# Output projection by halves of 512 columns, with the weights of a half kept for all token tiles

## The chip, the cores and the metric

The kernel runs on one core of a Trainium2 chip. The metric is the device time of one execution in microseconds; the time before is the median of three runs. The core has five engines: TensorE (PE in the profile, with PEld for its weight loads), VectorE (DVE), ScalarE (ACT), GpSimd (POOL) and SyncE (SP), which here issues most DMA transfers.

## What is computed

One layer of a diffusion backbone on 1280 tokens: 1024 latent tokens and 256 context tokens, each a row of 1024 numbers. All of it is float32. The part that matters, cut from the reference:

```
gates = sigmoid(br_pre).reshape(B, T, N_BRANCH, D_MODEL)
merged = sum(gates * branches, axis=2)
x = x + gt1 * (merged @ w_out)                      # output projection, 1024 x 1024
u2 = rmsnorm(x, g_norm2) * (1 + sc2) + sh2          # normalise rows, scale and shift columns
x = x + gt2 * (square(relu(u2 @ w_ff1)) @ w_ff2)    # feed-forward, 1024 -> 4096 -> 1024
```

`gt1`, `sc2`, `sh2` and `gt2` differ between latent and context tokens. Each float32 operand of a projection is split into two parts, high and low, and a product takes three matmuls: high x high, low x high, high x low.

## The kernel before

The tokens form ten tiles of 128 rows, in three groups: tiles 0 to 3 (group 0), 4 to 7 (group 1), both latent, and 8 and 9 (group 2, the context). A large buffer `z` of 20 pieces of 512 columns (`zs(0)` to `zs(19)`) holds the residual rows during the projection: tile i, called `xt[i]`, is `zs(2i)` and `zs(2i+1)`. In the feed-forward stage the same pieces hold weights and results, so a piece must have been stored (`scr_x`) and read by the normalising before it is overwritten.

Stages around the change, in order:

1. The merge (lines 963 to 993) sums three gated branches into `z`, and lines 1010 to 1016 split the sums into `mT[k][g]`, for eight blocks k of 128 columns and three groups.
2. `project_out(g, quarters)` multiplies a group with quarters of 256 columns of `w_out`. For each group and quarter anew, `out_weights` loads four halves of 256 KB and splits them (`load_half`: cast on ACT, subtraction on DVE); each holds two blocks k. A token tile of a quarter is 24 matmuls of 256 columns into one PSUM buffer `po` of three, then an eviction: a multiplication by the gate and an addition to the rows on DVE (lines 1090 and 1092), and a sum of squares on ACT (line 1093) into `fsq`. After the fourth quarter the tile is stored to `scr_x`.
3. `modulate_ff(g)` normalises a group: it adds up the squares (line 1039), takes the power -0.5 on POOL (line 131), scales the rows into `xn` (lines 1051 and 1053; six buffers `tmp2`, each for two tiles of a quarter), transposes them on PE (line 1059) and applies scale and shift. For latent groups this gives `u2r` (`raw2`), and splits `u2h` and `u2l`, which make up the quarter blocks B11, B21 (both of group 0) and B22; for group 2 it gives `u2c`.
4. The feed-forward's first product is done with a Strassen-like scheme of seven products for a pair of weight blocks (class `Pair`, 16 pairs). `begin` multiplies with B11 and B21 (two products, named `fB`, of 12 matmuls), `contexts` does the context tokens (48 matmuls of 256 columns, named `fc`), and `rest` multiplies with the sums T4, T2, T3, T1 (named `fT`) and with B22. `quarter_sums` forms these sums on DVE by 16 subtractions in place, and `split_sum` splits each of them.

The order before is: group 0 whole, a quarter of group 1, `modulate_ff(0)`, the rest of group 1, half of group 2, `modulate_ff(1)`, the quarter sums and the split of T4, the other half of group 2; then the begins of pairs 0 and 1, `modulate_ff(2)`, the other sums, the contexts.

The written order is only a priority. A planner with its own model of times places each instruction on its engine when its operands and a buffer are there in that model; on the chip each engine then runs its list in order. Buffers come from pools: 59 of 512 columns (`slot`), which hold `gt1` (4), `mT` (40) and later `u2r`, `u2h`, `u2l`, `u2c` and the split sums; six `six` and six `ring`, for high and low halves of weights; four `first4`; six `tmp2`. A buffer returns to its pool after its last reader.

Of the kernel before, what the change touches and what calls it, by code (L numbers as in the profile page):

```python
# [20 lines left out]
GROUPS = ((0, 512), (512, 512), (1024, 256))  # L21
# [28 lines left out]
def hybrid_step(  # L50
# [8 lines left out]
    V, A, G, PE = engines  # L59
    SP = nc.sync  # L60
# [15 lines left out]
    def ps_mm(name):  # L76
        return pp.tile([P, 512], F32, tag="mm", name=name, bufs=3)
# [79 lines left out]
    xt = [z[:, i * D : (i + 1) * D] for i in range(NT)]  # L157
# [90 lines left out]
    V, A, G, PE = (Pinned(tc, e) for e in engines)  # L248
# [73 lines left out]
    for g in range(3):  # L322
        t0, n = GROUPS[g]
# [91 lines left out]
    for g in range(3):  # L415
        t0, n = GROUPS[g]
# [291 lines left out]
    def quarter_sums(raw):  # L708
        for kk in range(4):
            b11, b21, b12, b22 = raw["B11"][kk], raw["B21"][kk], raw["B12"][kk], raw["B22"][kk]  # L710
            if raw is u_raw:
                for t, k, g in ((b11, kk, 0), (b12, kk, 1), (b22, kk + 4, 1), (b21, kk + 4, 0)):
                    SP.dma_start(t, scr_u[g][k])
            for out, x, y in ((b11, b12, b11), (b12, b22, b12), (b22, b22, b11), (b21, b22, b21)):
                V.tensor_tensor(out, x, y, ALU.subtract)

    def split_sum(dst, raw, nm):
        for kk in range(4):
            t = raw[SUMS[nm]][kk]
            if nm == "T2" and kk < 3:  # L720
                hi, lo = (six(f"t2{i}{kk}") for i in "hl")
            else:
                hi, lo = slot(f"{nm}h{kk}"), slot(f"{nm}l{kk}")
            A.copy(hi, t)
            V.tensor_tensor(lo, t, hi.bitcast(F32), ALU.subtract)
            dst[nm, kk] = hi, lo
# [87 lines left out]
    def load_half(src, name):  # L814

        raw = first4(f"raw_{name}", F32)
        SP.dma_start(raw, src)
        hi, lo = six(f"hi_{name}"), ring(f"lo_{name}")
        A.copy(hi, raw)  # L819
        V.tensor_tensor(lo, raw, hi.bitcast(F32), ALU.subtract)  # L820
        return hi, lo
# [141 lines left out]
    for ri, r in enumerate(ORDER):  # L963
        scr = (scr_ya, scr_yb, scr_yc)[r]
        ys = [[] for _ in range(4)]
        for g in range(3):
            for kc in range(4):
                t0, n = GROUPS[g]
# [4 lines left out]
        for d in range(KT):  # L973
            if d % 2 == 0:
                wb = [load_half(w_branch[r, d // 2][:, i * 512 : i * 512 + 512], f"wb{r}_{d}_{i}") for i in range(2)]
            for g in range(3):
                t0, n = GROUPS[g]
# [25 lines left out]
        return tl  # L1003

    gt1 = bcast_rows(0, "gt1")
    def out_weights(g, q):
        return [load_half(w_out[q, i // 2][:, i % 2 * 512 : i % 2 * 512 + 512], f"wo{g}{q}_{i}") for i in range(4)]

    first_out = out_weights(0, 0)
    mT = [[] for _ in range(KT)]  # L1010
    for g in range(3):
        for k in range(KT):
# [16 lines left out]
    raw2 = [[None] * KT for _ in range(2)]  # L1029
    u2s, u2c = {}, [None] * KT  # L1030
    scr_x = [dp.tile([P, D], F32, name=f"scr_x{i}") for i in range(NT)]

    fsq = cp.tile([P, NT, 4], F32, name="fsq")

    def modulate_ff(g):
        t0, n = GROUPS[g]
        tiles = range(t0 // P, (t0 + n) // P)
        fs = small([P, 4], f"fs{g}")[:, : len(tiles)]
        V.reduce_sum(fs, fsq[:, tiles[0] : tiles[-1] + 1, :], axis=mybir.AxisListType.X)
        r = rstd_of(fs, len(tiles), f"f{g}")  # L1040

        j = 1 if g == 2 else 0
        for qt in range(4):
            xn = []
            for ii, i in enumerate(tiles):
                if ii % 2 == 0:
                    t = tmp2(f"xn{i}_{qt}")
                v = t[:, (ii % 2) * 256 : (ii % 2) * 256 + 256]
                xv = xt[i][:, qt * 256 : (qt + 1) * 256]
                if ii % 2 == 0:  # L1050
                    A.activation(v, xv, AF.Copy, scale=r[:, ii : ii + 1])
                else:
                    V.tensor_scalar(v, xv, r[:, ii : ii + 1], None, ALU.mult)
                xn.append(v)
            for kk in range(2):
                k = qt * 2 + kk
                ps = ps_sd(f"pt2{g}_{k}")
                for ii in range(n // P):
                    PE.transpose(ps[:, ii * P : (ii + 1) * P], xn[ii][:, kk * P : (kk + 1) * P], ident)
                if g == 2:  # L1060
                    c = slot(f"u2{k}c")
                    u2c[k] = hi, lo = c[:, 0:256], c[:, 256:512]
                    A.activation(ps[:, :n], ps[:, :n], AF.Identity, bias=sh2[:, k, j : j + 1], scale=a2[:, k, j : j + 1])
                    V.tensor_copy(hi, ps[:, :n])
                    V.tensor_tensor(lo, ps[:, :n], hi.bitcast(F32), ALU.subtract)
                    continue
                rf = raw2[g][k] = slot(f"u2r{k}_{g}", F32)
                A.activation(rf, ps[:, :n], AF.Identity, bias=sh2[:, k, j : j + 1], scale=a2[:, k, j : j + 1])
                if g == 0 or k >= 4:
                    hi, lo = slot(f"u2h{k}_{g}"), slot(f"u2l{k}_{g}")  # L1070
                    V.tensor_copy(hi, rf)
                    V.tensor_tensor(lo, rf, hi.bitcast(F32), ALU.subtract)
                    u2s[f"B{1 + k // 4}{1 + g}", k % 4] = hi, lo

    def project_out(g, quarters=range(4)):
        t0, n = GROUPS[g]
        for q in quarters:
            wq = first_out if (g, q) == (0, 0) else out_weights(g, q)
            for i in range(t0 // P, (t0 + n) // P):
                o = i * P - t0  # L1080
                ps = ps_mm(f"po{q}_{i}")
                for k in range(KT):
                    whi, wlo = wq[k // 2]
                    s = slice((k % 2) * 256, (k % 2 + 1) * 256)
                    mh, ml = mT[k][g]
                    PE.matmul(ps[:, :256], mh[:, o : o + P], whi[:, s], start=k == 0, stop=False)  # L1086
                    PE.matmul(ps[:, :256], ml[:, o : o + P], whi[:, s], start=False, stop=False)  # L1087
                    PE.matmul(ps[:, :256], mh[:, o : o + P], wlo[:, s], start=False, stop=k == KT - 1)  # L1088
                gt = gt1[(2 if g == 2 else 0) + q // 2][:, (q % 2) * 256 : (q % 2) * 256 + 256]
                V.tensor_tensor(ps[:, :256], ps[:, :256], gt, ALU.mult)  # L1090
                xq = xt[i][:, q * 256 : (q + 1) * 256]
                V.tensor_tensor(xq, xq, ps[:, :256], ALU.add)  # L1092
                A.activation(ps[:, 256:512], xq, AF.Square, accum_out=fsq[:, i, q : q + 1])  # L1093
                if q == 3:
                    SP.dma_start(scr_x[i], xt[i])


    project_out(0)
    project_out(1, (0,))
    modulate_ff(0)  # L1100
    project_out(1, (1, 2, 3))
    project_out(2, (0, 1))
    modulate_ff(1)
    quarters = (("B11", 0, 0), ("B21", 0, 4), ("B12", 1, 0), ("B22", 1, 4))
    raw2q = {nm: raw2[g][o : o + 4] for nm, g, o in quarters}
    quarter_sums(raw2q)
    split_sum(u2s, raw2q, "T4")
    project_out(2, (2, 3))

# [47 lines left out]
    pairs = {}  # L1159

    def feed_pair(fp):
        odd = fp % 2
        pairs[fp] = FeedPair(
            f"{fp}", fp, (w_ff1[2 * fp], w_ff1[2 * fp + 1]), 4 if odd else 0, range(8, 12) if odd else range(12, 16), u2s, u2c)

    for fp in (0, 1):
        feed_pair(fp)
        pairs[fp].begin()
    modulate_ff(2)
    for nm in ("T3", "T2", "T1"):  # L1170
        split_sum(u2s, raw2q, nm)
    for fp in (0, 1):
# [174 lines left out]
def _layout(inputs):  # L1347
    import numpy as np

    f = {k: np.asarray(v) for k, v in inputs.items()}  # L1350
    a = {}
# [11 lines left out]
    s = np.arange(P)  # L1363
# [31 lines left out]
    a["w_gate"] = wgt.transpose(1, 0, 2)  # L1395
    a["bg"], a["m0"] = bg, m0
    a["w_branch"] = f["w_branch"][0].reshape(3, 4, P, 4, 256).transpose(0, 3, 2, 1, 4).reshape(3, 4, P, 1024)
    a["w_out"] = f["w_out"][0].reshape(2, 4, P, 4, 256).transpose(3, 0, 2, 1, 4).reshape(4, 2, P, 1024)
    a["w_ff1"] = f["w_ff1"][0].reshape(KT, P, NFF, P).transpose(2, 1, 0, 3).reshape(NFF, P, D)
    a["w_ff2"] = f["w_ff2"][0].reshape(NFF, P, D)  # L1400
    a["w_pool"] = f["w_pool"][0].transpose(1, 0, 2)
# [45 lines left out]
```

## Time and profile before

| what | value |
|---|---|
| median of three runs | 1984.17 us (1979.58 to 1986.23) |
| the profiled execution | 1989.21 us |
| its span, first to last instruction | 1987.4 us |
| PE busy | 1923.3 us, 97% |
| PEld busy | 1656.8 us, 83% |
| DVE busy | 1332.6 us, 67% |
| ACT busy | 858.1 us, 43% |
| mean granted TensorE clock | 0.989 |
| casts and subtractions of `w_out` | 48 of each, 28.8 us of ACT and 32.2 us of DVE |

"Busy" is the time in which an engine has an instruction under way. Matmuls overlap one another, so the pace of PE is read from the starts of successive instructions. The granted clock is the share of full speed that PE was given in a stretch. A bracket behind an instruction gives the idle time of its engine before it and what ended it. Times in rows are microseconds from the start of the span.

### The profile page before, as it was taken

The page shows a single profiled execution, that of the slowest core. Times are in us where ns is not written, and L with a number is a line of the kernel's source. Part 1 is how long each engine was busy: PE and PEld are TensorE (multiplying, and loading weights), DVE is VectorE, ACT ScalarE, POOL GpSimd, SP SyncE. Part 2 cuts the span into 40 slices and gives each one's busy share as a digit, 9 for nine tenths or more (in the row PEclk, how much of TensorE's full clock was granted, in tenths as well). Part 3 has the DMA queues.
Part 4 walks back from the last instruction along what each step waited for, and adds up shares of the span by engine and source line. Part 5 has one row for each costly group of instructions (what it writes and reads, how often), then busy time and mean ns, then how long its engine had stood idle before and what let it go on. Part 6 is the DMA issues. An engine that isn't in the chain of part 4 may idle for free. (4 is left out here: it accounts for less than half of the span.)

```text
span 1987.4 us, 29215 instructions
## 1 busy us (share of the span) xinstructions
PE 1923.3 (97%) x10544; PEld 1656.8 (83%) x10544; DVE 1332.6 (67%) x2269; ACT 858.1 (43%) x1780; POOL 382.5 (19%) x372
## 2 busy tenths in 40 slices
PE   5999999999899999999999999999999999999997
PEld 2788888998778888878889998888888878888886
DVE  6684344448878979774566689888776654654664
ACT  6543454653143333331014565554445544443443
POOL 3000001116402324330000005445441110000002
PEclk9999999999999999999999998999999999999999
DMA  8211111112564545469634535776774586655544
GB/s 341 86 45 38 48 59 42 40 57 85 175 228 145 169 142 176 133 210 345 234 122 149 170 139 186 271 260 237 249 275 142 190 324 210 197 177 155 165 134 148
DMA packets 160642, 332.70 MB, mean 167 GB/s; under 512 B 18929, under 2 KB 41329, under 8 KB 158449
## 3 DMA queue, kind: packets, MB, share of 16 engines
q1 hardware_dynamic: 107280, 224.30, 34.6%
q10 hardware_dynamic: 38976, 52.97, 7.4%
q0 software_dynamic: 14240, 53.56, 7.3%
q8 instruction: 83, 1.36, 0.3%
q14 instruction: 63, 0.51, 0.1%
HBM read 229.53 MB, written 101.22 MB: 166 GB/s over the span
## 5 line engine op out<-in xcount | busy, mean ns | idle before, releaser
L1155 POOL TENSOR_TENSOR z<-z 128x512 f32<-128x512 f32 x64 | 98.7, 1543 | 133.7 <-DMA z<-in_w_ff 131.0
L885 DVE TENSOR_TENSOR z<-z 128x512 f32<-128x512 f32 x112 | 92.2, 824 | 2.5
L445 POOL PARTITION_ALL_REDUCE acc<-acc x16 | 55.0, 3474 | 188.5 <-DVE acc L439 117.6
L439 DVE SCALAR_TENSOR_TENSOR acc<-z,scond,acc 128x512 f32<-128x512 f32 x112 | 85.9, 815 | 0.0
L1269 POOL TENSOR_TENSOR rs_y<-rs_y,neghalf 128x1 f32<-128x1 f32 x10 | 9.4, 940 | 333.6 <-DVE rs_y L1268 333.6
L1121 ACT ACTIVATE z<-z 128x512 f32<-128x512 f32 x64 | 40.5, 632 | 76.4 <-DVE z L894 36.7
L910 ACT ACTIVATE z<-z 128x512 f32<-128x512 f32 x48 | 30.2, 632 | 71.8 <-DVE z L894 27.7
L819 ACT CAST hi_wb<-raw_wb 128x512 fp32r<-128x512 f32 x24 | 14.8, 620 | 100.7 <-PE pb L987 67.2
L131 POOL TENSOR_TENSOR rs_h<-rs_h,neghalf 128x4 f32<-128x4 f32 (+1 forms) x12 | 11.9, 992 | 207.9 <-DVE rs_h L130 207.8
L992 DVE TENSOR_TENSOR sg<-pb,sg 128x512 f32<-128x512 f32 (+1 forms) x48 | 28.9, 602 | 33.0 <-PE pb L988 31.6
L582 DVE SCALAR_TENSOR_TENSOR yc<-th,ccol,z 128x512 f32<-128x512 f32 (+1 forms) x12 | 7.9, 660 | 57.2 <-PE th L580 57.2
L1122 ACT ACTIVATE z<-z 128x512 f32<-128x512 f32 x64 | 40.3, 630 | 1.1
L670 POOL TENSOR_TENSOR z<-z 128x1024 f32<-128x1024 f32 (+13 forms) x20 | 34.8, 1750 | 14.0 <-ACT z L654 12.5
L819 ACT CAST hi_wo<-raw_wo 128x512 fp32r<-128x512 f32 x48 | 28.8, 616 | 19.9 <-PE po L1087 13.6
L1090 DVE TENSOR_TENSOR po<-po,gt 128x256 f32<-128x256 f32 x40 | 17.2, 430 | 29.3 <-PE po L1088 29.2
L1146 POOL DMA_DIRECT2D scr_s<-x x48 | 26.3, 551 | 52.0 <-DVE x L1140 47.3
L446 POOL TENSOR_TENSOR acc<-acc,bt 1x512 f32<-1x512 f32 x16 | 23.8, 1500 | 59.0 <-issue 59.0
L820 DVE TENSOR_TENSOR lo_wo<-raw_wo,hi_wo 128x512 fp32r<-128x512 f32 x48 | 32.2, 686 | 3.6 <-ACT hi_wo L819 3.6
L44 PE MATMUL pm<-wah,shl 128*4 128x512 f32 x32 | 14.7, 479 | 17.2 <-DVE s_x L44 12.5
L1093 ACT ACTIVATE po<-z 128x256 f32<-128x256 f32 x40 | 15.4, 385 | 36.9 <-DVE z L1092 35.7
L516 DVE SCALAR_TENSOR_TENSOR z<-z,dmb,kv 128x129 f32<-128x129 f32 x56 | 16.3, 344 | 21.9 <-PE kv L505 21.6
L569 DVE TENSOR_TENSOR den<-den,gcol 128x2 f32<-128x2 f32 x40 | 6.2, 159 | 35.2 <-ACT den L568 34.4
(5091 smaller groups left out, 7466.7 us busy)
## 6 DMA issues: line engine op xcount, KB each, us to landing
z<-in_w_ff SPq DMA_DIRECT2D x64, 512.0 KB, 5.5
z<-in_w_ada SPq DMA_DIRECT2D x64, 256.0 KB, 3.3
scr_t<-z POOLq DMA_DIRECT2D x16, 1024.0 KB, 4.6
z<-in_w_in SPq DMA_DIRECT2D x24, 512.0 KB, 4.4
scr_g<-z ACTq DMA_DIRECT2D x48, 256.0 KB, 2.0
sg<-scr_g SPq DMA_DIRECT2D x48, 256.0 KB, 4.6
raw_wo<-in_w_out SPq DMA_DIRECT2D x48, 256.0 KB, 3.5
scr_h<-z ACTq DMA_DIRECT2D x48, 256.0 KB, 4.0
```

The source lines that it names most:

```text
L439: V.scalar_tensor_tensor(acc[j], raw, scond[:, k, j : j + 1], acc[j], ALU.mult, ALU.add)
L445: G.partition_all_reduce(acc[j], acc[j], P, bass.bass_isa.ReduceOp.add)
L670: eng.tensor_tensor(at(dst, a, b), at(src, a - l, b - l), at(src, a + r_, b + r_), ALU.add)
L819: A.copy(hi, raw)
L820: V.tensor_tensor(lo, raw, hi.bitcast(F32), ALU.subtract)
L885: V.tensor_tensor(out, x, y, op)
L910: A.activation(t, t, AF.Sigmoid)
L992: V.tensor_tensor(sg[:, :n], pb[:, :n], sg[:, :n], ALU.mult)
L1121: A.activation(t, t, AF.Relu)
L1122: A.activation(t, t, AF.Square)
L1146: G.dma_start(scr_s[fp][:, i, :], t)
L1155: G.tensor_tensor(out, x, y, ALU.subtract)
```

## The change

The projection is cut into two halves of 512 columns instead of quarters of 256. All eight blocks of a half are loaded and split once, and stay for all ten token tiles: 16 loads of 256 KB instead of 48. A tile of a half is 24 matmuls of 512 columns. The array `w_out` is laid out to match.

The blocks of the first half lie in `six`, `ring` and `first4`, those of the second in eight slots (k below 4) and again in `six` and `ring`; the raw weights pass through `tmp2`. The order becomes: half 0 of tiles 0 to 9, half 1 of tiles 0 to 4, `modulate_ff(0)`, half 1 of tiles 5 to 9; then `begin` of pair 0, `modulate_ff(1)`, `begin` of pair 1, `modulate_ff(2)`, the quarter sums and all four split sums, the contexts.

In `z`, even pairs now use pieces 0 to 3 for weights and 4 to 7 for results (group 0's rows), odd pairs 8 to 11 and 12 to 15 (group 1's rows). Before, weights of pairs 0 and 1 lay in group 0's pieces and their results in group 1's. `FREE`, the order in which the second product takes pieces over, is changed to suit.

```diff
-    def out_weights(g, q):
-        return [load_half(w_out[q, i // 2][:, i % 2 * 512 : i % 2 * 512 + 512], f"wo{g}{q}_{i}") for i in range(4)]
-    first_out = out_weights(0, 0)
+    def out_weights(hf, ks=range(KT)):
+        ws = []
+        for k in ks:
+            raw = tmp2(f"raw_wo{hf}_{k}")
+            SP.dma_start(raw, w_out[hf, k])
+            if hf == 0:
+                rooms = (six, ring) if k < 6 else (first4, first4)
+            else:
+                rooms = (slot, slot) if k < 4 else (six, ring)
+            hi, lo = (room(f"{x}_wo{hf}_{k}") for room, x in zip(rooms, ("hi", "lo")))
+            A.copy(hi, raw)
+            V.tensor_tensor(lo, raw, hi.bitcast(F32), ALU.subtract)
+            ws.append((hi, lo))
+        return ws
+    w_out0 = out_weights(0)
...
-    def project_out(g, quarters=range(4)):
-        ...
+    def project_out(hf, wo, tiles):
+        for i in tiles:
+            g = min(i // 4, 2)
+            o = i * P - GROUPS[g][0]
+            ps = ps_mm(f"po{hf}_{i}")
+            for k in range(KT):
+                whi, wlo = wo[k]
+                mh, ml = mT[k][g]
+                PE.matmul(ps, mh[:, o : o + P], whi, start=k == 0, stop=False)
+                PE.matmul(ps, ml[:, o : o + P], whi, start=False, stop=False)
+                PE.matmul(ps, mh[:, o : o + P], wlo, start=False, stop=k == KT - 1)
+            V.tensor_tensor(ps, ps, gt1[(2 if g == 2 else 0) + hf], ALU.mult)
+            xh = xt[i][:, hf * 512 : hf * 512 + 512]
+            V.tensor_tensor(xh, xh, ps, ALU.add)
+            A.activation(ps, xh, AF.Square, accum_out=fsq[:, i, hf : hf + 1])
+            if hf == 1:
+                SP.dma_start(scr_x[i], xt[i])
-    project_out(0)
-    project_out(1, (0,))
+    project_out(0, w_out0, range(8))
+    w_out1 = out_weights(1, range(4))
+    project_out(0, w_out0, (8, 9))
+    w_out1 += out_weights(1, range(4, KT))
+    project_out(1, w_out1, range(5))
     modulate_ff(0)
-    project_out(1, (1, 2, 3))
-    project_out(2, (0, 1))
-    modulate_ff(1)
-    quarters = ...
-    quarter_sums(raw2q)
-    split_sum(u2s, raw2q, "T4")
-    project_out(2, (2, 3))
+    project_out(1, w_out1, range(5, 10))
...
-            ..., 4 if odd else 0, range(8, 12) if odd else range(12, 16), u2s, u2c)
-    for fp in (0, 1):
-        feed_pair(fp)
-        pairs[fp].begin()
+            ..., 8 if odd else 0, range(12, 16) if odd else range(4, 8), u2s, u2c)
+    feed_pair(0)
+    pairs[0].begin()
+    modulate_ff(1)
+    quarters = ...
+    feed_pair(1)
+    pairs[1].begin()
     modulate_ff(2)
+    quarter_sums(raw2q)
+    split_sum(u2s, raw2q, "T4")
     for nm in ("T3", "T2", "T1"):
         split_sum(u2s, raw2q, nm)
-    FREE = (0, 2, 16, 18, 12, 14, 4, 6, 8, 10)
+    FREE = (0, 2, 16, 18, 4, 6, 8, 10, 12, 14)
-    a["w_out"] = ....reshape(2, 4, P, 4, 256).transpose(3, 0, 2, 1, 4).reshape(4, 2, P, 1024)
+    a["w_out"] = ....reshape(KT, P, 2, 512).transpose(2, 0, 1, 3)
```

More of the change, by code (lines that the diff above doesn't have):

```diff
@@ L1038, in modulate_ff @@
         fs = small([P, 4], f"fs{g}")[:, : len(tiles)]
-        V.reduce_sum(fs, fsq[:, tiles[0] : tiles[-1] + 1, :], axis=mybir.AxisListType.X)
+        V.reduce_sum(fs, fsq[:, tiles[0] : tiles[-1] + 1, 0:2], axis=mybir.AxisListType.X)
         r = rstd_of(fs, len(tiles), f"f{g}")
@@ L1073, in modulate_ff @@
                     u2s[f"B{1 + k // 4}{1 + g}", k % 4] = hi, lo
-    def project_out(g, quarters=range(4)):
[L1076 to L1095, printed above, removed]
@@ L1098, in hybrid_step @@
-    project_out(0)
-    project_out(1, (0,))
-    modulate_ff(0)
-    project_out(1, (1, 2, 3))
-    project_out(2, (0, 1))
-    modulate_ff(1)
-    quarters = (("B11", 0, 0), ("B21", 0, 4), ("B12", 1, 0), ("B22", 1, 4))
-    raw2q = {nm: raw2[g][o : o + 4] for nm, g, o in quarters}
-    quarter_sums(raw2q)
-    split_sum(u2s, raw2q, "T4")
-    project_out(2, (2, 3))
+    def project_out(hf, wo, tiles):
[15 more added lines that the diff above has]
+                SP.dma_start(scr_x[i], xt[i])
@@ L1163, in feed_pair @@
         pairs[fp] = FeedPair(
-            f"{fp}", fp, (w_ff1[2 * fp], w_ff1[2 * fp + 1]), 4 if odd else 0, range(8, 12) if odd else range(12, 16), u2s, u2c)
-    for fp in (0, 1):
-        feed_pair(fp)
-        pairs[fp].begin()
+            f"{fp}", fp, (w_ff1[2 * fp], w_ff1[2 * fp + 1]), 8 if odd else 0, range(12, 16) if odd else range(4, 8), u2s, u2c)
+    feed_pair(0)
+    pairs[0].begin()
+    modulate_ff(1)
+    quarters = (("B11", 0, 0), ("B21", 0, 4), ("B12", 1, 0), ("B22", 1, 4))
+    raw2q = {nm: raw2[g][o : o + 4] for nm, g, o in quarters}
+    feed_pair(1)
+    pairs[1].begin()
     modulate_ff(2)
+    quarter_sums(raw2q)
+    split_sum(u2s, raw2q, "T4")
     for nm in ("T3", "T2", "T1"):
@@ L1397, in _layout @@
     a["w_branch"] = f["w_branch"][0].reshape(3, 4, P, 4, 256).transpose(0, 3, 2, 1, 4).reshape(3, 4, P, 1024)
-    a["w_out"] = f["w_out"][0].reshape(2, 4, P, 4, 256).transpose(3, 0, 2, 1, 4).reshape(4, 2, P, 1024)
+    a["w_out"] = f["w_out"][0].reshape(KT, P, 2, 512).transpose(2, 0, 1, 3)
     a["w_ff1"] = f["w_ff1"][0].reshape(KT, P, NFF, P).transpose(2, 1, 0, 3).reshape(NFF, P, D)
```

## The prediction

> **What bounds the kernel now.** I read the totals of the page first, then the stages of the trace around the output projection, and then TensorE (PE) instruction by instruction where a stage shows less than full work.
>
> ```profile
> span 1987.4 us, 29215 instructions
> PE 1923.3 (97%) x10544; PEld 1656.8 (83%) x10544; DVE 1332.6 (67%) x2269; ACT 858.1 (43%) x1780; POOL 382.5 (19%) x372
> ...
> core 0: us, PE busy (x) PEld busy (x) DVE busy (x) ACT busy (x) POOL busy (x), PEclk, DMA share, GB/s
> 1040.00:1060.00 20.00, 20.00 (x116) 17.65 (x115) 14.97 (x26) 7.08 (x13) 1.58 (x3) 1.00 0.27 79
> 1080.00:1100.00 20.00, 20.00 (x169) 20.00 (x169) 10.86 (x23) 7.59 (x22) 0.00 (x0) 1.00 0.41 132
> 1160.00:1180.00 20.00, 20.00 (x172) 20.00 (x171) 18.73 (x41) 17.00 (x38) 0.00 (x0) 1.00 0.27 90
> 1180.00:1200.00 20.00, 15.89 (x73) 13.03 (x72) 18.30 (x41) 14.19 (x30) 1.67 (x1) 0.86 0.33 117
> 1200.00:1220.00 20.00, 19.65 (x123) 18.42 (x122) 18.96 (x37) 12.90 (x27) 10.85 (x6) 0.88 0.40 145
> ```
>
> PE is busy 97% of the span, so time can go only where PE gets fewer microseconds of work, or where it idles or runs slowly. Both occur here. Through the projection (1060 to 1180) PE has no gap, and weight loads (PEld) fill all 20 us of a stage, unlike before it (17.65). At 1180 to 1220 PE has its only hole hereabouts, VectorE (DVE) is nearly full (18 to 19 of 20 us) and the granted clock falls to 0.86 and 0.88.
>
> The next rows are single PE instructions in order of time: start, duration, name.
>
> ```profile
> 1057.66 0.28 PE L1086 MATMUL po<-hi_wo,m0h 128*128 128x256 f32 x1
> ...
> 1175.09 0.28 PE L1086 MATMUL po<-hi_wo,m0c 128*128 128x256 f32 x1
> 1180.73 0.28 PE L1088 MATMUL po<-lo_wo,m7c 128*128 128x256 f32 x1
> 1180.85 0.40 PE L828 MATMUL fB<-u2h,a_0h 128*128 128x512 f32 x1
> 1191.53 0.39 PE L830 MATMUL fB<-u2h,a_1l 128*128 128x512 f32 x1
> 1195.66 2.39 PE L1059 MATMUL pt<-cst,xn 128*128 128x128 f32 x10 [3.74 <-ACT xn L1051]
> 1217.04 0.40 PE L828 MATMUL fT<-t2h,s_0h 128*128 128x512 f32 x1
> ```
>
> Between 1175.09 and 1180.73 lie 47 steps without a gap: 0.120 us per 256-column matmul. Between 1180.85 and 1191.53 lie 47 steps: 0.227 us per 512-column one. The bracket is the hole: PE waited 3.74 us for the normalised rows `xn` of the third token group. What the clock did then:
>
> ```profile
> 1190.00:1195.00 5.00, 1.92 (x9) 1.26 (x7) 4.51 (x10) 3.87 (x7) 1.61 (x1) 0.96 0.14 52
> 1195.00:1200.00 5.00, 3.97 (x16) 3.35 (x17) 3.80 (x12) 4.59 (x11) 0.06 (x1) 0.50 0.66 205
> 1200.00:1205.00 5.00, 5.00 (x26) 5.00 (x25) 3.96 (x12) 2.24 (x5) 3.32 (x3) 0.52 0.15 61
> 1205.00:1210.00 5.00, 4.65 (x37) 4.36 (x36) 5.00 (x6) 4.21 (x10) 2.76 (x3) 1.00 0.28 120
> ```
>
> After the hole the clock stays near 0.5 for about 10 us: 26 instructions where the next 5 us hold 37. The Trainium skill, page "TensorE: Matmul & The Clock Gate", section "Part 1: The HAM clock gate", gives half clock after an idle window of about 3.4 us; the 3.74 us row agrees.
>
> Why the rows came late, in rows of DVE, ScalarE (ACT) and GpSimd (POOL):
>
> ```profile
> 1186.74 0.41 DVE L1092 TENSOR_TENSOR z<-z,po 128x256 f32<-128x256 f32 x1
> 1187.38 0.38 ACT L1093 ACTIVATE po<-z 128x256 f32<-128x256 f32 x1
> 1190.68 0.15 DVE L1039 TENSOR_REDUCE fs<-fsq 128x2 f32<-128x8 f32 x1
> 1193.16 0.16 DVE L130 TENSOR_SCALAR rs_f<-fs 128x2 f32<-128x2 f32 x1
> 1193.39 1.68 POOL rs_f L131
> ```
>
> The last projection matmul starts at 1180.73, but its addition comes 6 us later, the sum of squares waits until 1190.68 and the 0.16 us scaling until 1193.16. DVE is full of quarter sums and splits planned in between.
>
> **The loss of the old tail.** From 1057.66 to 1217.04, 159.4 us, PE does 960 projection matmuls (115.2 at 0.120), 80 transposes at 0.109 (20 take 2.18, row below; 8.7), 48 matmuls of the pairs' first two products (10.9 at 0.227), 96 of the context parts (256 columns, 11.5) and 12 of the T4 product (2.7): 149.0. So 10.4 us are lost: 3.7 in the hole, about 4 to the slow clock, the rest in sub-microsecond waits and switches.
>
> ```profile
> 1116.47 2.18 PE pt L1059 x20
> ...
> 1057.40:1217.03 159.63, 117.97 (x960) 115.90 (x960) 33.67 (x80) 20.34 (x80) 0.97 0.47 161
> 1057.40:1217.03 159.63, 12.76 (x80) 10.23 (x80) 5.75 (x16) 15.79 (x24) 0.97 0.47 161
> 1057.40:1217.03 159.63, 15.28 (x96) 14.50 (x96) 1.15 (x3) 0.97 0.47 161
> 1057.40:1217.03 159.63, 3.36 (x12) 2.16 (x13) 0.00 (x0) 0.58 (x1) 0.97 0.47 161
> ```
>
> (Each row counts one kind of product: projection, transposes, context, T products.)
>
> **The change, part by part.**
>
> Columns: 960 matmuls of 256 become 480 of 512. 115.2 minus 480 x 0.2272 (109.1) is 6.1 us, all on PE, which has no gap there. This is the safest term. Its ends are 5 and 7 us, from reading the steps as 0.118 to 0.120 and 0.226 to 0.228. The clock page's section "Back-to-back issue gap" states another price: columns / 2.4 GHz plus 2.5 ns, thus 109.2 and 215.8 ns, so 480 x 2.5 ns, 1.2 us by estimate. The rows show 13 to 14 ns per matmul beyond the columns instead of 2.5, at both widths, so I stay with the rows.
>
> Weights: 48 loads of 256 KB with a split each become 16.
>
> ```profile
> L819 ACT CAST hi_wo<-raw_wo 128x512 fp32r<-128x512 f32 x48 | 28.8, 616 | 19.9 <-PE po L1087 13.6
> L820 DVE TENSOR_TENSOR lo_wo<-raw_wo,hi_wo 128x512 fp32r<-128x512 f32 x48 | 32.2, 686 | 3.6 <-ACT hi_wo L819 3.6
> L1090 DVE TENSOR_TENSOR po<-po,gt 128x256 f32<-128x256 f32 x40 | 17.2, 430 | 29.3 <-PE po L1088 29.2
> ```
>
> That frees 19.2 us of ACT and 21.5 of DVE, and 8 MB of transfers on SP's queue. Under a full PE this is worth nothing by itself; it pays where DVE was full. Evictions go from 40 of 256 to 20 of 512 columns, three buffers deep, under 5.45 us of matmuls per tile (24 x 0.227): nothing, as about 2.3 us of chain fits thrice. If that cover went, each tile would show a wait of up to 1 us.
>
> Start of the stage: two of the eight first weights (k = 4, 5) take buffers which the merge frees only at its end, 1057.6, and k = 4 is needed 12 x 0.227 = 2.7 us later. A cast (0.62) and a subtraction (0.69) each, in parallel on two engines, take about 2 us, but DVE is 15 of 20 us busy then. Bounds 0 to 2 us; I take 0.5, since the planner can start a second tile meanwhile. The second half's k = 4 to 7 reuse the buffers of k = 0 to 3, free after tile 9 has read each: 5.45 us tile, then 2.7, against four splits at 0.69: hidden, price 0 to 1.
>
> Group 0's normalising moves to about 1137 (14 tiles of 5.45 us from 1057.7, then an eviction and the statistics), under the five remaining tiles (27 us): hidden. Pair 0's weights follow it; before, all four feed-forward loads went out early:
>
> ```profile
> 1119.27 1.43 SPq L843 DMA_DIRECT2D z<-in_w_ff  x3
> 1159.69 2.50 ACT L1051 ACTIVATE xn<-z,rs_f 128x256 f32<-128x256 f32 x6
> 1169.23 0.50 ACT L1051 ACTIVATE xn<-z,rs_f 128x256 f32<-128x256 f32 x1
> z<-in_w_ff SPq DMA_DIRECT2D x64, 512.0 KB, 5.5
> ```
>
> The tail is where I choose. The projection now ends near 1057.7 + 109.1 + 3.5 (32 transposes) + 1 = 1171. Tile 7 ends about 11 us before that (tiles 8 and 9), so group 1's rows are ready near 1164.5, 7 us ahead of the end, where before it was 1159 against 1181. Pair 1's weights now land in tiles 4 and 5, so they wait for group 1's last `xn`. That one was 9.5 us after the first before (1159.69 against 1169.23), since it needs a buffer that a transpose frees. So they issue at 1174 to 1177 and land 5.5 us later, 1180 to 1183, behind tile 9's store on SP; split by 1184.
>
> PE's work free of the T sums after 1171: two begins (10.9), 48 transposes (5.2), contexts (11.5), 27.6 us, to 1198.6. In it pair 0's begin and the transposes last to about 1181, and contexts of pair 0 wait on group 2's parts, so a hole of 1 to 3 us before pair 1's weights is likely. DVE's work until T4's halves are ready, with starts 0.60 us apart for 512 columns and 0.33 for 256:
>
> ```profile
> 1176.40 1.21 DVE u2r L715 x2
> 1177.60 0.60 DVE a_1l L811
> 1198.62 0.41 DVE L1065 TENSOR_TENSOR u20c<-pt,u20c 128x256 fp32r<-128x256 f32 x1
> 1198.95 0.41 DVE L1064 CAST u22c<-pt 128x256 fp32r<-128x256 f32 x1
> ```
>
> 16 quarter sums 9.6, T4 2.4, pair splits 8 x 0.6, their two additions 1.2, group 1's second-half parts 3.7, group 2's 16 x 0.33 = 5.3, rows 3.2, tile 9's addition 1.2: 31.4 us. From 1164.5 without a pause that is 1195.9, before 1198.6; with some 5 us of pause while group 1's transposes stand behind pair 0's begin it is 1201. So T4 costs PE 0 to 6 us; I take 2, as most of the operands are there early. New losses: 0.5 at the start, 2 there, 1 before pair 1, 1 of switches, 4.5 against 10.4: a gain of 5.9. The half clock goes if no hole reaches the 3.7 us of before.
>
> The order of the quarters in the second stage (`FREE`) only follows the new places of the last pairs' data: 0.
>
> **Sum.** 6.1 + 5.9 = 12.0 us off PE's path. The profiled execution took 1989.2 us (span 1987.4 and 1.8 around it), thus 1977.2; it lies 5 us above the median 1984.17 of the three runs, so for the median I say 1972.
>
> **Rivals.** (A) The columns pay, the tail does not: T4 or pair 1's weights leave a hole of 4 to 6 us with the slow clock after it, 4 more, so about 10 are lost as before. For it: DVE full until 1220. Against: DVE has 21.5 us less of weight splits. Time 1984.2 minus 6 = 1978; with two such holes 1984. (B) A 512-column step costs two of 256: the columns bring nothing and only the tail's 5.9 us stay, 1978. Against it stand the two measured steps, each over 47 matmuls. The skill's issue gap is this case with 1.2 us left, 1977 by estimate.
>
> (C) Slower. Group 1's chain moved from 22 to 7 us ahead of the projection's end, and quarter sums and T4 moved behind it and group 2. If DVE's 31.4 us start only once pair 0's begin and the transposes are over, and are kept in an order that puts group 2's late parts first, T4 slides. It decides when T4 comes later than about 1215: a hole of 16.5 us plus 5 of slow clock and 1 elsewhere make 22.5, 12.1 more than the old loss, minus 6.1: 6 us slower, 1990. Speaking against it: 1176 plus all 31.4 is only 1207. (D) Nothing in the tail is lost: 2 us left, gain 14.5, 1969.5.
>
> **How the numbers follow.** Forecast (a tail loss of 3 to 7 us) 0.45, D 0.17, A 0.25, B 0.05, C 0.08. About 6 us (0.3%) is what a measurement tells from no change. Faster by more: forecast, D, B and a third of A, 0.75; within: most of A, 0.17; slower: C, 0.08. The range is 1964 (D with 5 us of spread between runs, which 1979.58 to 1986.23 show) to 1985 (A with two holes); C is left out. The forecast's own range is 1968 to 1977.
>
> **What would show it.** Projection steps of 0.227 us, 480 of them, and an end near 1171. No idle over 3 us at 1170 to 1210 and granted clock 1.00 there; the first T4 product at about 1200; DVE still full to about 1210. It is wrong if PE shows a wait for pair 1's weights, `u2c` or T4 of over 4 us with half clock behind it, or per-tile waits at `po`.

## The result and the profile after

The changed kernel takes 1992.01 us (median of 6 runs, 1986.71 to 1996.13) against 1983.54 before: a ratio of 1.0048, 95% interval 1.0029 to 1.0067, some 9 us slower. The forecast was 1972.

Page totals of the changed kernel; below them its work in stretches of 20 us, with the columns of the prediction's second fence:

```profile
span 1987.8 us, 27987 instructions
PE 1915.7 (96%) x10064; PEld 1626.2 (82%) x10064; DVE 1306.2 (66%) x2197; ACT 834.2 (42%) x1708; POOL 386.0 (19%) x372
...
1160.00:1180.00 20.00, 16.20 (x84) 12.96 (x82) 11.09 (x24) 12.04 (x26) 0.69 (x1) 0.95 0.40 147
1180.00:1200.00 20.00, 15.11 (x67) 12.38 (x67) 19.93 (x39) 10.96 (x21) 13.10 (x5) 0.71 0.24 91
1200.00:1220.00 20.00, 16.47 (x100) 13.64 (x100) 19.96 (x29) 12.94 (x28) 8.30 (x6) 1.00 0.49 173
```

The profiled spans, 1987.8 and 1987.4, are alike because the program's front, ahead of the projection, varies by several microseconds between runs. So I count from the first projection matmul. Single PE instructions after the change:

```profile
1053.15 0.40 PE L1098 MATMUL po<-hi_wo,m0h 128*128 128x512 f32 x1
...
1165.61 0.39 PE L828 MATMUL fB<-u2h,a_0h 128*128 128x512 f32 x1
1171.06 2.78 PE L1073 MATMUL pt<-cst,xn 128*128 128x128 f32 x24
1179.12 0.80 PE L828 MATMUL fB<-u2h,a_1h 128*128 128x512 f32 x1 [3.29 <-ACT a_1h L810]
1194.58 0.66 PE L1073 MATMUL pt<-cst,xn 128*128 128x128 f32 x2 [2.54 <-DVE u20c L1079]
1213.44 0.46 PE L828 MATMUL fT<-t2h,s_0h 128*128 128x512 f32 x1
```

The projection did what was forecast: 112.5 us from 1053.15 to 1165.61 for 480 matmuls at 0.227 (109.0) and 32 transposes (3.5), without a wait. Yet the first T2 product comes 160.3 us after the start of the stage, where before it came after 159.4. The whole gain went in the 48 us between the projection's end and that product, called the tail here.

All PE work from the first projection matmul to that T2 product, then the longest waits of PE in the tail (total, times, longest):

```profile
1053.15:1213.44 160.29, 149.64 (x719) 124.54 (x717) 96.67 (x177) 66.50 (x144) 26.37 (x19) 0.96 0.28 102
```

```profile
PE fB L828 <- ACT a_1h L810: 3.3, 1, 3.3
PE pt L1073 <- DVE u20c L1079: 2.5, 1, 2.5
PE fc L830 <- DVE a_1l L811: 1.6, 1, 1.6
PE pt L1073 <- DVE z L865: 1.4, 1, 1.4
PE fc L828 <- DVE u20c L1078: 0.9, 1, 0.9
```

PE idles 10.65 us of 160.29. Its work at full pace, by the prediction's prices, is 142.8 (109.0 for the projection, 33.8 as before for the rest), so 6.8 more go to the slow clock and to switches: a loss of 17.5 us, against 10.4 before. The clock (column behind POOL's) in stretches of 5 us:

```profile
1175.00:1180.00 5.00, 1.53 (x6) 0.92 (x6) 4.07 (x7) 5.00 (x11) 0.00 (x0) 0.78 0.82 297
1180.00:1185.00 5.00, 5.00 (x14) 3.69 (x14) 5.00 (x10) 3.21 (x6) 2.49 (x1) 0.53 0.31 98
1190.00:1195.00 5.00, 1.06 (x5) 0.70 (x5) 5.00 (x8) 1.69 (x3) 4.76 (x4) 0.65 0.14 52
1195.00:1200.00 5.00, 5.00 (x32) 5.00 (x31) 4.93 (x13) 2.48 (x5) 0.84 (x2) 0.67 0.52 213
```

Two holes, at 1176 and at 1190, and behind each about 5 us at half to two thirds of the clock. The rows of the other engines say why:

```profile
1158.69 1.67 DVE L1067 TENSOR_SCALAR xn<-z,rs_f 128x256 f32<-128x256 f32 x6 [1.12 <-POOL rs_f L131]
1165.81 0.70 DVE L1101 TENSOR_TENSOR po<-po,gt 128x512 f32<-128x512 f32 x1 [4.02 <-PE po L1100]
1171.31 0.69 DVE L865 TENSOR_TENSOR z<-z,fB 128x512 f32<-128x512 f32 x1 [2.87 <-PE fB L830]
1172.34 0.89 SPq L843 DMA_DIRECT2D z<-in_w_ff  x2
1178.45 0.62 ACT L810 CAST a_1h<-z 128x512 fp32r<-128x512 f32 x1
1192.68 1.41 DVE L715 TENSOR_TENSOR u2r<-u2r,u2r 128x512 f32<-128x512 f32 x1
1194.02 0.41 DVE L1079 TENSOR_TENSOR u20c<-pt,u20c 128x256 fp32r<-128x256 f32 x1
1201.39 1.89 DVE L725 TENSOR_TENSOR T4l<-u2r,T4h 128x512 fp32r<-128x512 f32 x3
```

Group 1's first rows are ready at 1158.7, but PE has their transposes (`pt`) behind tile 9 and pair 0's first products, until 1171.06. DVE idles 4.0 and 2.9 us meanwhile. Then all comes at once. Pair 1's weights are asked for at 1172.34 and the first of them land 3.6 us later, at 1175.9; but ACT, busy without a pause from 1171.7, has rows of group 1 and pair 0's results ahead of their cast in its list and reaches it at 1178.45 (the first hole). From 1171.3 to T4's last low half at 1203.3 DVE works without a pause of over 0.4 us, with quarter sums (`u2r`) standing ahead of the low half of `u20c` that PE's next transposes need a buffer from (the second hole).

Behind 1213.44 the changed kernel loses 4.1 us more up to the first product of the second feed-forward stage (1593.90 against 1593.45 before, so 380.5 us instead of 376.4). Of its holes there the largest stems from a late store on POOL's queue:

```profile
1252.73 0.58 ACT L862 COPY z<-fB 128x512 f32<-128x512 f32 x1 [7.70 <-DMA scr_s<-z]
...
1253.88 0.50 PE L828 MATMUL fT<-t2h,s_2h 128*128 128x512 f32 x1 [2.23 <-ACT s_2h L810]
```

ACT's copy for pair 2 waits 7.7 us until pair 0's sums in that piece are stored, and the cast `s_2h` stands behind it in ACT's list.

From the first projection matmul to the second stage the two traces thus differ by 5.0 us, where the medians differ by 8.5. The execution that was profiled before took 1989.21 us, 5.7 above its kernel's median; where the other 3 to 4 us lie no trace shows.

### The profile page after: what moved, and what is told of

It is laid out like the page before. It is cut to its first block, busy times and chain, and to the rows that moved or that the text cites. A ratio compares the mean times of both kernels' runs of the same rounds, so it can differ in the third digit from the quotient of the medians.

```text
span 1987.8 us, 27987 instructions
## 1 busy us (share of the span) xinstructions
PE 1915.7 (96%) x10064; PEld 1626.2 (82%) x10064; DVE 1306.2 (66%) x2197; ACT 834.2 (42%) x1708; POOL 386.0 (19%) x372
## 4 chain that ended last, share of the span: by engine, by line
PE 77%; DVE 7%; DMA 6%; POOL 4%; issue 3%; ACT 2%; SPq 0%; ACTq 0%; POOLq 0%; DVEq 0%
PE w L1328 6%; PE w L1329 6%; PE w L1330 6%; PE pb L988 3%; PE pb L986 3%; PE pb L987 3%; PE fT L830 2%; PE fT L828 2%; PE fT L829 2%; PE fB L830 2%; PE fB L829 2%; PE fB L828 2%; PE po L1100 2%; PE po L1098 2%; PE po L1099 2%
## 5 line engine op out<-in xcount | busy, mean ns | idle before, releaser
L1162 POOL TENSOR_TENSOR z<-z 128x512 f32<-128x512 f32 x64 | 102.8, 1606 | 139.3 <-DMA z<-in_w_ff 136.2
L992 DVE TENSOR_TENSOR sg<-pb,sg 128x512 f32<-128x512 f32 (+1 forms) x48 | 28.7, 600 | 31.5 <-PE pb L988 31.4
L1101 DVE TENSOR_TENSOR po<-po,gt 128x512 f32<-128x512 f32 x20 | 14.0, 698 | 50.5 <-PE po L1100 50.4
L1104 ACT ACTIVATE po<-z 128x512 f32<-128x512 f32 x20 | 12.0, 600 | 67.5 <-DVE z L1103 40.2
L993 DVE TENSOR_TENSOR z<-z,sg 128x512 f32<-128x512 f32 (+1 forms) x48 | 28.8, 601 | 1.3
L44 PE MATMUL pm<-wah,shl 128*4 128x512 f32 x32 | 14.6, 470 | 15.4 <-ACT wah L44 15.3
L990 DVE TENSOR_TENSOR z<-pb,sg 128x512 f32<-128x512 f32 (+1 forms) x24 | 14.0, 598 | 20.9 <-PE pb L988 18.4
```

What stands on the lines that cost most here:

```text
L1162: G.tensor_tensor(out, x, y, ALU.subtract)
```

## The experiments

Each kernel was timed in five rounds beside the kernel before. "Shift" is the ratio's distance from 1 times 1983 us. The expectations name their theories by letters. O: the changed order loses, since group 1's chain starts late and all that follows it is late. P: POOL's second sums (subtractions for the second product's weights), which now start 129.4 us after the first projection matmul instead of 143.9, slow DVE. Q: the halves themselves bring nothing. R, formed when O and P had failed alone: PE arrives earlier, but the tail is as long as DVE's serial work in it. L: the new places of the pairs' data carry the loss.

| kernel | ratio, 95% interval | shift, us |
|---|---|---|
| changed | 1.0048 (1.0029 to 1.0067) | +9.5 |
| norm1_first | 1.0043 (1.0027 to 1.0058) | +8.5 |
| pool_held | 1.0040 (1.0028 to 1.0053) | +7.9 |
| columns_alone | 1.0002 (0.9993 to 1.0011) | +0.4 |
| order_alone | 1.0077 (1.0061 to 1.0093) | +15.3 |
| columns_sums_last | 0.9992 (0.9980 to 1.0004) | -1.6 |
| columns_pool_held | 0.9979 (0.9967 to 0.9990) | -4.2 |
| columns_both | 0.9990 (0.9980 to 1.0000) | -2.0 |
| columns_new_pieces | 1.0026 (1.0015 to 1.0037) | +5.2 |
| changed_old_pieces | 1.0032 (1.0019 to 1.0044) | +6.3 |
| changed_no_sums | 0.9997 (0.9988 to 1.0006) | -0.6 |
| before_no_sums | 0.9977 (0.9968 to 0.9986) | -4.6 |
| columns_no_sums | 0.9972 (0.9963 to 0.9981) | -5.6 |
| columns_no_sums_last | 0.9983 (0.9974 to 0.9992) | -3.4 |
| quarters_context_first | 0.9990 (0.9981 to 0.9999) | -2.0 |
| context_first | 0.9944 (0.9932 to 0.9957) | -11.1 |

### Which part loses: the columns or the order

columns_alone has the halves with the old order behind them and the old places; order_alone has the quarters with the changed order and places.

```
# columns_alone, against the changed kernel
-    project_out(1, w_out1, range(5, 10))
+    project_out(1, w_out1, range(5, 8))
+    modulate_ff(1)
...  # quarters, raw2q
+    quarter_sums(raw2q)
+    split_sum(u2s, raw2q, "T4")
+    project_out(1, w_out1, (8, 9))
...  # begins of pairs 0 and 1 together behind it, old pieces, old FREE
# order_alone, against the kernel before; then the changed kernel's tail, pieces and FREE
-    project_out(2, (0, 1))
-    modulate_ff(1)
...
-    project_out(2, (2, 3))
+    project_out(2)
```

> The first part of the change alone: halves of 512 columns with the weights kept, but the tail in the order of the kernel before (group 1's normalising, quarter sums and T4 ahead of the last two token tiles, pieces of z as before). Theory O: the columns' 6.1 us come through: 1976 to 1979 us against 1983.5 before; with the freed VectorE time also shortening the old hole, down to 1972. Theory P: the same 1977, since GpSimd starts late again. Theory Q (the columns do not pay, whatever the tail): 1983 us.

> The second part of the change alone: quarters of 256 columns as before (48 weight loads), but the tail in the changed order and with the changed pieces of z. Theory O: the order costs what the changed kernel lost beyond the columns, 8.5 + 6.1 = 14.6 us: 1996 to 1999 us; less, about 1990, if the earlier end of group 1 (27 instead of 11 us ahead of the projection's end) lets its transposes slip in. Theory Q: the loss belongs to the halves, 1984 us.

Order and places without the columns cost 15.3 us; with the columns on top (the changed kernel) it is 9.5, so the columns gave about the 6 they were priced at (the intervals leave some 5 us of room on either side). In the old order the same columns gave nothing, +0.4. PE's and DVE's rows in columns_alone show where they went:

```profile
1191.99 0.58 PE L828 MATMUL fc<-u20c,a_0h 128*128 128x256 f32 x1 [10.16 <-DVE u20c L1078]
```

```profile
1180.65 0.69 DVE L865 TENSOR_TENSOR z<-z,fB 128x512 f32<-128x512 f32 x1
1181.24 1.55 DVE L1086 TENSOR_TENSOR u2l<-u2r,u2h 128x512 fp32r<-128x512 f32 x1
1182.72 1.75 DVE L725 TENSOR_TENSOR T4l<-u2r,T4h 128x512 fp32r<-128x512 f32 x1
1184.40 1.75 DVE L715 TENSOR_TENSOR u2r<-u2r,u2r 128x512 f32<-128x512 f32 x1
1186.07 1.75 DVE L725 TENSOR_TENSOR T4l<-u2r,T4h 128x512 fp32r<-128x512 f32 x1
...
1191.52 0.42 DVE L1078 CAST u20c<-pt 128x256 fp32r<-128x256 f32 x1
```

PE ends the projection 7 us earlier after its start (115.9 us with 64 transposes, instead of 123.2) and then waits 10.16 us, in one piece, for the first context part. Its cast stands in DVE's list behind sums and splits, and four of those take 1.55 to 1.75 us each instead of 0.68, for this reason:

```profile
1180.98 6.29 POOL L1168 TENSOR_TENSOR z<-z 128x512 f32<-128x512 f32 x4 [5.29 <-DMA z<-in_w_ff]
```

While POOL subtracts, from 1180.98 to 1187.3, DVE steps with both operands in SBUF (the tiles and `z`; `po`, `pt`, `fB` and `fc` lie in PSUM) are slow, and steps of 0.68 us surround them. The Trainium skill, page "SBUF — State Buffer", section "Who interferes with whom", states that such a DVE instruction and a GpSimd one that reads SBUF exclude each other; 0.68 plus up to one POOL step (6.29 / 4 = 1.6) covers the 1.75, so these rows agree.

### Holding POOL off, and group 1 first

```
# norm1_first, against the changed kernel
-    pairs[0].begin()
     modulate_ff(1)
+    pairs[0].begin()
# pool_held (changed kernel) and columns_pool_held (columns_alone): the second sums' first loads behind T4
+        if fp == 0:
+            for at in (16, 18):
+                A.copy(zs(at)[:, 0:1], u2s["T4", 3][1][:, 0:1].bitcast(F32))
```

> The changed kernel (1992.0 us) with group 1's normalising written ahead of the begin of pair 0, so that its 32 transposes stand before, not behind, the 24 matmuls of that begin on TensorE; all else as changed. Theory O (order in the tail: group 1's transposes wait behind pair 0's begin, and pair 1's weights and the quarter sums wait with them): transposes at about 113 us after the first projection matmul instead of 118, pair 1's weights 5 us earlier, the 3.3 us hole and the half clock after it gone: 6 to 9 us less, 1983 to 1986 us, same as before. Theory P (GpSimd's first subtractions of the second product now start 22 us earlier and slow VectorE just where it is last): nothing of that is moved, 1990 to 1993 us.

> The changed kernel (1992.0 us) with GpSimd's first subtractions for the second product (pair 0) held until T4 is split, by two one-column copies on ScalarE into the place where their operands are loaded. Theory P: VectorE's steps of 1.1 to 1.8 us between 1189 and 1211 fall back to 0.6, group 2's parts and the T sums come about 6 us earlier: 1984 to 1987 us. Theory O: the holes of 3.3 us ahead of it stay, at most 2 us gained: 1990 to 1992 us; it can be slower if GpSimd's work slides into the pairs.

> The columns alone (1981.4 us), with GpSimd's first subtractions held until T4 is split. Theory P (sharing with GpSimd): the four VectorE steps of 1.55 to 1.75 us at 1181 to 1188 take 0.60 again, u2c comes 4.3 us earlier, and with less of the half clock: 1974 to 1977 us. Theory R without P (order alone counts): within 2 us, 1980 to 1983 us.

Both edits of the changed kernel bring at most 2 us, within the intervals: neither theory holds alone. The 3.3 us hole went in norm1_first, but others took its place; in pool_held it stayed and a later one appeared. Waits of PE in norm1_first, then in pool_held:

```profile
PE fc L828 <- DVE u20c L1078: 6.9, 1, 6.9
PE fB L828 <- ACT s_1h L810: 5.2, 1, 5.2
```

```profile
PE fB L828 <- ACT s_1h L810: 4.2, 1, 4.2
PE fB L828 <- ACT a_1h L810: 3.3, 1, 3.3
```

In columns_pool_held the hole shrank from 10.2 to 6.7 us and the shift is -4.2: there POOL's part is shown, about 4 us (the intervals leave 2 to 8).

### DVE's list, and its volume

columns_sums_last moves the quarter sums and T4's split of columns_alone behind `modulate_ff(2)`; columns_both adds the hold on POOL.

> The columns alone (1981.4 us, with a hole of 10.2 us before group 2's context part), with one change of order: the quarter sums and the split of T4 are written behind group 2's normalising instead of ahead of the last two tiles. Theory R (the tail belongs to VectorE's fixed list, in which 11 sums and splits stand between group 2's rows and the first cast of u2c): that cast comes about 10 us earlier, the hole shrinks to 1 to 3 us and its half clock goes, some of it comes back as a wait for T4: 1971 to 1976 us. Theory O (what costs is sums behind the normalising, as in the changed kernel): slower than the columns alone, 1984 to 1990 us.

> The columns alone with both: sums behind group 2's normalising, GpSimd held until T4 is split. Theory R and P together: 1969 to 1973 us. If only one of them counts, no better than the better of the two single runs, within 2 us.

Both miss: reordering DVE's list moved the hole (4.3 us for `u20c`'s low half in columns_sums_last, 3.7 for `s_1h` in columns_both) and did not close it. So next the volume. `quarter_sums(raw2q)` is left out, so that the T products take other operands, in the changed kernel, the kernel before and columns_alone:

> The changed kernel without the 16 quarter sums (left out: the 16 DVE subtractions of 128x512 ahead of T4, so the T products take other operands; every other instruction stays). 16 x 0.6 to 0.7 us, 9.6 to 11 us, of DVE leave the tail. Theory R (DVE's serial work between group 1's rows and the parts sets the tail's end; PE idles for it): 1981 to 1985 us, 7 to 11 less than the changed kernel. Rival (the tail waits for when things start, for transfers and PE's own order, not for DVE's volume): 1989 to 1992 us.

> The kernel before with the same 16 quarter sums left out, the control for changed_no_sums. Theory R says that the old tail has DVE slack under the longer projection, with only the 3.7 us hole and its slow clock to win: 1976 to 1982 us, 2 to 7 less than before. If the same 7 to 11 us go here as in changed_no_sums, DVE's volume binds both alike and does not explain why the change lost: 1973 to 1977 us.

> The halves with the old order (columns_alone) without the 16 quarter sums (the same 16 DVE subtractions left out as in before_no_sums). It asks where the 6 us of the columns went. Theory R (they are there, and a PE that arrives 7 us earlier only waits for DVE): with 10 us less on DVE the 10.2 us hole shrinks to 2 us or less and the columns show in full, 1970 to 1974 us, 5 to 8 below before_no_sums. Rival B (wide matmuls bring nothing, or something outside the tail takes it): 1976 to 1980 us, as before_no_sums.

Ten microseconds less on DVE take 10.1 us off the changed kernel (+9.5 to -0.6; the intervals leave 6 to 14) and 4.6 off the kernel before (3 to 6). The traces, one of each, do not bear the difference out: from the first projection matmul to the second stage's first product they give 540.8 us with and 533.9 without the sums in the changed kernel, 535.8 and 528.2 before, thus 6.9 and 7.6 less; and in the changed kernel only 2.5 of it comes ahead of the first T2 product. So DVE's volume costs both kernels time, but that it binds the changed tail more than the old one is not shown. columns_no_sums is a miss: -5.6, only 1.0 below before_no_sums, where theory R wanted 5 to 8. Its rows:

```profile
1183.55 2.35 DVE L725 TENSOR_TENSOR T4l<-u2r,T4h 128x512 fp32r<-128x512 f32 x2
1187.07 0.69 DVE L725 TENSOR_TENSOR T4l<-u2r,T4h 128x512 fp32r<-128x512 f32 x1 [1.17 <-ACT T4h L724]
1187.68 0.42 DVE L1078 CAST u20c<-pt 128x256 fp32r<-128x256 f32 x1
```

DVE is no longer full, but `u20c` still stands behind T4's split, which itself waits for ACT, and PE waits 4.03 us. The last run of this line moves T4's split away too:

> columns_sums_last (halves, old order, T4's split behind group 2's parts; 1981.7 us) without the 16 quarter sums (left out). In columns_no_sums PE still waited 4.0 us for the first context part u20c, whose cast stood in DVE's list behind T4's split. Theory R2 (what swallows the columns is DVE's list: its volume, and T4's split ahead of the context parts in it): 1971 to 1974 us, the columns' 6 us below before_no_sums (1978.3). Rival (something outside DVE keeps the tail): 1976 to 1980 us.

Another miss (-3.4), and the most instructive one. Up to 1215 PE has no long wait left; its first T4 product comes 136 us after the stage's start (143 in before_no_sums). Then the next queue ends the gain:

```profile
1217.81 0.90 SPq L1163 DMA_DIRECT2D z<-in_w_ff  x2
1218.79 9.96 SPq L843 DMA_DIRECT2D z<-in_w_ff  x2
```

```profile
1197.16 15.60 POOL L1166 TENSOR_TENSOR z<-z 128x512 f32<-128x512 f32 x4 [7.11 <-DMA z<-in_w_ff]
1213.05 0.57 POOL L1167 DMA_DIRECT2D scr_t<-z  x1 [0.30 <-POOL z L1166]
```

```profile
1224.44 0.62 ACT L810 CAST a_2h<-z 128x512 fp32r<-128x512 f32 x1 [10.32 <-DMA z<-in_w_ff]
...
1225.63 0.79 PE L828 MATMUL fT<-T1h,s_1h 128*128 128x512 f32 x1 [4.17 <-ACT s_1h L810]
```

Half of pair 2's weights is issued on SP at 1218.79, behind loads for POOL's next sums (L1163), whose pieces are free only when POOL has stored the last ones, a store issued at 1213.05; those took 15.60 us for four subtractions. ACT holds at their cast for 10.3 us, pair 1's cast `s_1h` stands behind it, and PE idles 4.2 us. PE arrived earlier than a transfer that nothing had made earlier.

### The places of the pairs' data

```
# columns_new_pieces, against columns_alone (changed_old_pieces is the reverse, on the changed kernel)
-            ..., 4 if odd else 0, range(8, 12) if odd else range(12, 16), u2s, u2c)
+            ..., 8 if odd else 0, range(12, 16) if odd else range(4, 8), u2s, u2c)
-    FREE = (0, 2, 16, 18, 12, 14, 4, 6, 8, 10)
+    FREE = (0, 2, 16, 18, 4, 6, 8, 10, 12, 14)
```

> The kernel with the halves and the old order behind the projection (columns_alone, 1981.4 us) with one thing added: the changed places of the pairs' data (pair 1's weights in z pieces 8 to 11, the pairs' result pieces 4 to 7 and 12 to 15, FREE to match). Theory L (the places carry the loss, since loads and casts in them wait for stores that are issued late): 1988 to 1992 us. Theory O (the order carries it, the places nothing): 1980 to 1983 us, as columns_alone.

> The changed kernel with its order kept and the old places of the pairs' data put back (pair 1's weights in z pieces 4 to 7, results 12 to 15 and 8 to 11, old FREE). The fourth corner of order by places. Theory L: 1981 to 1985 us, most of the changed kernel's loss against columns_alone is gone. Theory O: 1990 to 1993 us, nothing changes.

In changed_old_pieces pair 0's first results overwrite token tile 6 before group 1 is normalised, so group 1's values differ, and its normalising has to wait for those results: ACT's `xn` goes on at 1177.9, right behind pair 0's last step there, and PE waits 2.3 us for it. The four corners are +0.4 (old order, old places), +5.2 (old, new), +6.3 (new, old) and +9.5 (new, new). The places cost about 5 us in the old order. The third corner has that wait on top, so the order's own price is at most about 6 us there, and what the places cost in the new order stays open. The largest wait of PE behind the tail in columns_new_pieces is the queue of the last section again:

```profile
1200.12 24.90 SPq L1165 DMA_DIRECT2D z<-in_w_ff  x4
1225.07 0.90 SPq L843 DMA_DIRECT2D z<-in_w_ff  x2
```

```profile
1231.42 0.62 ACT L810 CAST a_2h<-z 128x512 fp32r<-128x512 f32 x1 [13.77 <-DMA z<-in_w_ff]
...
1232.62 0.79 PE L828 MATMUL fT<-T3h,s_1h 128*128 128x512 f32 x1 [4.96 <-ACT s_1h L810]
```

Pair 2's weights go out at 1225.07 and ACT is held 13.8 us; in columns_alone the last of them goes out at 1217.9 and no such wait shows. Why the planner put them behind the second sums' loads with these places was not tried.

### An order that uses the columns

context_first projects group 2 ahead of the last tiles of group 1, so its context parts are ready early and PE has the pairs' context products as cover; group 1's sums and T4 come last. Pair 0's results lie in pieces 16 to 19, which also keeps the second sums' loads, and with them POOL, back; the other pairs have the old places. quarters_context_first has the same order and places with quarters.

```
# context_first, against the changed kernel
-    project_out(1, w_out1, range(5))
+    project_out(1, w_out1, (0, 1, 2, 3, 8, 9))
     modulate_ff(0)
-    project_out(1, w_out1, range(5, 10))
+    project_out(1, w_out1, (4,))
+    modulate_ff(2)
+    project_out(1, w_out1, (5, 6, 7))
...
     pairs[0].begin()
+    feed_pair(1)
     modulate_ff(1)
...  # raw2q
-    feed_pair(1)
     pairs[1].begin()
-    modulate_ff(2)
     quarter_sums(raw2q)
     split_sum(u2s, raw2q, "T4")
...  # old places and FREE, but pair 0's results in range(16, 20)
```

> Halves of 512 columns, with the context tiles 8 and 9 of the second half ahead of tiles 4 to 7: group 2 is normalised under the projection, pair 0's results lie in the context's pieces 16 to 19 (so GpSimd's first subtractions start only after pair 0), pair 1's weights in group 0's pieces, and the quarter sums come last. Theory R: the contexts (11.5 us of PE) are free of waits and cover group 1's chain of 26 us on VectorE together with the two begins: losses of 3 to 5 us instead of 10.4, 1969 to 1973 us. Theory O (group 1's normalising behind the begin of pair 0 is itself what costs): 1984 us or more.

> The kernel before, quarters of 256 columns, with the order of context_first: group 2 projected ahead of group 1, its rows normalised between group 1's quarters, group 1's chain behind pair 0's first products, quarter sums and T4 behind that. It parts what the columns and what the order gave in context_first (1972.05 us). If the columns' 6 us are real and only hidden by the tail: 1977 to 1980 us. If the order gives all and the columns nothing: 1971 to 1974 us. If the order helps only with wide columns: 1982 us or more.

context_first takes 1972.05 us (1970.49 to 1975.38), below both kernels. Order and places alone give 2.0 of its 11.1 us; the halves give the other 9.1 (6 to 12). That is more than the 6 us of PE work, and which part the weight splits saved on DVE and ACT have in it was not tried. Stretches of 20 us in context_first:

```profile
1160.00:1180.00 20.00, 20.00 (x125) 17.86 (x125) 13.94 (x33) 13.77 (x28) 1.01 (x1) 1.00 0.17 66
1180.00:1200.00 20.00, 17.74 (x104) 14.44 (x102) 20.00 (x37) 12.69 (x26) 0.00 (x0) 1.00 0.12 39
1200.00:1220.00 20.00, 17.89 (x64) 13.66 (x65) 16.70 (x29) 12.08 (x22) 0.77 (x1) 0.83 0.24 80
```

DVE is as full at 1180 to 1200 as in the changed kernel, but POOL is silent beside it, and PE has work that does not wait for it: 4.4 us of idle at 1160 to 1220 instead of 12.2.

## Why the prediction was wrong

- **Columns.** Right: 480 steps of 0.227 us, no wait in the stage. Forecast 6.1 us off PE, measured 6.2 as work (115.2 against 109.0); order_alone against the changed kernel gives 5.8. Rival B falls. The issue gap of the Trainium skill's page "TensorE: Matmul & The Clock Gate" (section "Back-to-back issue gap"), which the page gives for a single isolated matmul, would by estimate have saved 1.2 us; the 6.2 us measured disagree.
- **Weights, evictions, start of the stage, group 0.** Priced at nothing or 0.5; no wait shows. Right.
- **The tail.** This step failed. It was to lose 4.5 us and lost 17.5, with 4 more behind it; in the quarters the same order and places cost 15.3 in all. Some of it came as forecast: with the first projection matmul 4.5 us earlier than in the row the prediction started from, its "pair 1's weights issue at 1174 to 1177" is 1169.5 to 1172.5 here, and they went out at 1172.34; the hole ahead of them, seen as 1 to 3 us and charged with 1, was 3.3; T4, charged with 2, cost 0.4. Two terms were wrong. I charged PE for T4, the end of DVE's list, and nothing for steps in its middle: the parts of group 2, an addition for pair 1 and a split of pair 1, each behind quarter sums or splits, cost PE 4.9 us at 1188 to 1195 and 1.6 at 1212. And the slow clock and switches, charged with 1 us because no hole was to reach 3.7, took 6.8.
- **When DVE's list starts.** It was to start at 1160 in this run's time, with a pause of 5 us; but for six rows `xn` and two evictions it began at 1171.3, since group 1's transposes stood behind tile 9 and pair 0's begin, so T4 came at 1203.3 instead of 1191.5 to 1196.5. From there the list took 32.0 us (1171.31 to 1203.3), near the "31.4 us" of the prediction partly by luck: four of the eight pair splits, tile 9's addition and those six rows lie outside it, and three low halves of T2 and some 2 us of slower steps beside POOL lie inside.
- **Rival C.** It named this late start. Its 1990 lies near the 1992 by luck: its hole of 16.5 us ahead of a T4 later than about 1215 (1210.5 in this run's time) never came; the loss came in shorter holes with T4 at 1203.
- **The second hole's price.** Slow clock after a hole of 3.3 us was rival A's price (4 us); it came twice. Behind a wait of 3.29 us the clock stood at 0.53 for 5 us. The Trainium skill, page "TensorE: Matmul & The Clock Gate", section "Part 1: The HAM clock gate", gives about 3.4 us for the idle window behind which the clock is halved; this row is a little under it.
- **Weight splits.** "DVE has 21.5 us less", held against rival A, was true of the program, but little of it helped the tail: before, 9 of the 48 lay between 1160 and 1176 (6.1 us) and the others ahead of that, where DVE had room; and in the changed kernel DVE idles 4.0 and 2.9 us at 1161 to 1171, waiting for PE.
- **Places, `FREE`.** Priced 0. The new places cost about 5 us in the old order, through SP's queue and ACT's list. I had counted which buffers become free, not which loads stand ahead of which on SP.
- **What POOL does to DVE.** Not in the sum; about 4 us in columns_pool_held, and 1.6, within the interval, in pool_held.

Not settled: how the 15 us of order and places divide among the late group 1, POOL and the queues, since each edit alone moved the hole elsewhere. What the columns are worth depends on the tail behind them: +0.4 us in the old order, -5.8 in the changed one, -9.1 in context_first's. In the first, PE's wait of 10.16 us shows where they went. That cover by independent work decides it is argued, not shown: the changed order has no such cover, and the columns paid there.

## What to carry to other kernels

Time taken off the busiest engine ahead of a narrow place can be worth nothing, as in columns_alone, where PE only waits longer for DVE: before pricing it, list in order what the next engine has ahead of each operand that PE will ask for, not only of the last one. When removing one wait only brings up another of the same size, try to put independent work there (as context_first does with the context products) rather than only a better order of the late engine's list. A weight load is as early as the loads ahead of it on its queue, so price a change of buffers by each queue's order too.

## What the runs showed of the hardware

- DVE steps of 128x512 with both operands in SBUF took 0.68 us alone and 1.55 to 1.75 us beside POOL's subtractions in columns_alone. Four of these subtractions took 6.29 us there, 15.60 in columns_no_sums_last, and 12.71 in the changed kernel, where DVE kept its 0.68 us for the first 6 us of them, so that here POOL was held up:

```profile
1182.51 12.71 POOL L1162 TENSOR_TENSOR z<-z 128x512 f32<-128x512 f32 x4 [13.29 <-DMA z<-in_w_ff]
```

- DVE steps that read PSUM kept their time in the same stretch: 0.41 us for `u20c<-pt,u20c` at 1194.02, between steps of 1.4.
- A wait of ACT for a transfer is a wait of all that stands behind it: 10 to 14 us of waiting for `a_2h` became 4 to 5 us of idle PE.
